# A two-model chain on one core: TensorE's queue written out by hand up to the retention stage, and attention's steps in another order

## The chip, the cores and the metric

The kernel runs on one core of one Trainium2 chip. A core has a matrix engine (TensorE, PE in the profile, with its weight loads as PEld), VectorE (DVE), ScalarE (ACT), GpSimd (POOL) and SyncE (SP), which here only issues the DMA transfers of weights. Each engine works its own queue in the order in which it was given, and waits at an instruction until what it needs is there. The metric is the device time of one execution in microseconds; less is better.

## The reference, cut to what matters

256 positions of 1024 numbers go through ten stages, all in fp32. Seven of them have a name that the text uses: f00, f01, f10, f11 (the feed-forward halves of the first model), conv, attention, and retention and f20 of the second model.

```python
for l in range(DEPTH):                     # DEPTH = 2
    g = norm_g[l]
    if l == N_A_LAYERS:                    # N_A_LAYERS = 1
        k, v = shared_kv(h, kv_norm_g, w_kv)
    h = h + 0.5 * rmsnorm(swiglu(rmsnorm(h, g[0]), ffn_w_gu[l, 0], ffn_w_down[l, 0]), g[1])
    xn = rmsnorm(h, g[2])
    if l < N_A_LAYERS:
        mix = short_gated_conv(xn, conv_w_in[l], conv_k[l], conv_w_out[l])
    else:
        mix = diff_attention(xn, k, v, attn_w_q[j], attn_lambda[j], attn_subln_g[j], attn_w_o[j], lambda_init)
    h = h + rmsnorm(mix, g[3])
    h = h + 0.5 * rmsnorm(swiglu(rmsnorm(h, g[4]), ffn_w_gu[l, 1], ffn_w_down[l, 1]), g[5])
# second model, on the result x of the first
x = x + retention(rms_norm(x, mix_norm[0]), ret_w_in[0], ret_out_norm[0], ret_w_o[0])
x = x + swiglu_2(rms_norm(x, ffn_norm[0]), ffn_w_in[0], ffn_w_out[0])
x = x + stick_breaking(rms_norm(x, mix_norm[1]), sb_w_in[0], sb_q_norm[0], sb_k_norm[0], sb_w_o[0])
x = x + swiglu_2(rms_norm(x, ffn_norm[1]), ffn_w_in[1], ffn_w_out[1])
```

In diff_attention each of 8 heads has two softmaxes; their difference weighs the values v, the result is normed per head and projected by w_o.

## The kernel before, in words

The 256 rows stand in SBUF as two halves h[0] and h[1] of 128 rows, called A and B here. All weights stream in as units of 1 MB. A unit is loaded raw by a DMA on SP's queue (three raw buffers), then split by `Weights.split` into two parts: ACT casts it to `whi` and DVE subtracts to `wlo`, each in two pieces of 128x1024. Five pairs of parts can be held. An fp32 product is made of three matmuls (whi by xT's high part, wlo by the high part, whi by the low part), lines L274 to L276 where weights stand as columns, L297 to L303 in the projections that accumulate rows (`acc`), L487 and L490 in the feed-forward's input projection `whole`. Twelve matmuls of 512 columns on one half of the rows and half a unit are called a step.

The order on PE, ACT and DVE is that of a scheduler that builds each engine's queue from the source, from its own estimates of when data are ready; only a few pieces are marked `manual_schedule` and stand as written: part of the opening, and ACT in stage 8.

Between two stages `boundary` runs: the previous stage's last steps for half A, then `chain_A[0]` (the update of h: squares on ACT, `y` on DVE L387 and L389, a power on POOL L392, `h` on DVE L394), two of the last steps for half B, `chain_A[1]` (eight transposes `tr_x` of h on PE L338 in two groups of four, which ACT L321 and DVE L323 turn into the parts xT), the last steps for B, `chain_B[0]`, some steps of the new stage for half A, `chain_B[1]`, and the rest.

In the feed-forward stages `tr(c, half)` transposes the hidden row block (`tr_h` L520; ACT and DVE make the parts hT), and `across` turns the norm factors into a row: DVE copies `spread` (L358), PE transposes it (`tr_r` L359), ACT copies `rows`. Both borrow PSUM buffers of the accumulators.

In attention `vp` projects values (four steps of it for each half), `s1` makes scores `sc` and their maxima `nm`, `s2` the exponentials `s` on ACT (L831), `s3` the weighted difference aA (half A) or aB (half B), `pv1` transposes it (`tr` on PE, `aT` on ACT L864), `pv2` multiplies with v (`tr_o` or `mm`, L874) and norms to `yo`, `tr_o` transposes that into the parts `xk` (ACT L897, DVE L898) for the output projection `out`.

Of the kernel before, what the change touches and what calls it, by code (L numbers as in the profile page):

```python
# [194 lines left out]
def tile_two_models(ctx: ExitStack, tc: tile.TileContext, a: dict):  # L195
# [66 lines left out]
    borrowed = []  # L262
# [139 lines left out]

    def boundary(prev_tail, chain_A, chain_B, head_A, head_B, few):
        for s in prev_tail[0]:
            s()
            W.pump(1)
        chain_A[0]()
        for s in prev_tail[1][:2]:  # L410
            s()
        chain_A[1]()
        if few:
            W.pump(1)
        for s in prev_tail[1][2:]:
            s()
        chain_B[0]()
        W.pump(1)
        n = 3 if few == 2 else 2
        for s in head_A[:n]:  # L420
            s()
        chain_B[1]()
        W.pump(1)
        for s in head_A[n:]:
            s()
            W.pump(1)
        for s in head_B:
            s()
            W.pump(1)

    def ffn(tag, xT, rstd, skew=True, first=None, last_stage=False, opening=False):
# [7 lines left out]
        def gu(c, half, j, last=True):  # L439
            if j == 0:  # L440
                gu_ps[c, half] = new_mm()
            mm_col(gu_ps[c, half], xT[half], (tag, "gu", c), j, last)
            if j == 1:
                evict(c, half)
# [69 lines left out]
        def tr(c, half):  # L514
            if c not in hT:
                hT[c] = k4.tile([P, 2, 2, 2, P], F32R, tag="k4", name=f"hT{c}")
            t = new_tr("tr_h")
            src = hid.pop((c, half))
            for k in range(2):
                T.transpose(t[:, k * P : k * P + P], src[:, k * P : k * P + P], ident)  # L520
            split_plain(t[:, 0:256].rearrange("p (k t) -> p k t", k=2), hT[c][:, half, 0], hT[c][:, half, 1])
# [22 lines left out]
        def body():  # L544
            nonlocal first
            if opening:
                for j in range(2):
                    by_tile(0, j)
                    W.pump()
                for j in range(2):  # L550
                    for half in range(2):
                        gu(1, half, j, last=half == 1)
                    W.pump()
                    for half in range(2):
                        borrowed.append(half)
                        if j == 0:
                            tr(0, half)
                        elif half == 0:
                            across(rstd)
                            acc.update(factors(rstd))  # L560
                        borrowed.pop()
            for c in range(2 if skew or opening else 0, NCH):
                for j in range(2):
                    whole(c, j)
                    borrowed.append(0)
                    if first is not None:
                        first()
                        first = None
                    if opening and c == 2 and j == 0:
                        tr(1, 0)  # L570
                        borrowed[-1] = 1
                        tr(1, 1)
                    if skew and c == 2 and j == 0:
                        tr(1, 1)
                    borrowed[-1] = 1
                    if not opening and c == (2 if skew else 0) and j == 0:
                        across(rstd)
                        acc.update(factors(rstd))
                    borrowed.pop()
                    W.pump()  # L580
                if 2 <= c < NCH - 1:
                    for half in range(2):
                        dn(c - 2, half, last=half == 1)
                    W.pump()
# [183 lines left out]
    def attention(xT, rstd, xk, rstd_k, kT):  # L768
# [154 lines left out]

        def body():
            vp(2, 0, 0)
            tr_q(1, 1)
            vp(2, 1, 0)
            W.pump(1)
            s1(0, 1)
            vp(2, 0, 1)  # L930
            s2(0, 1)
            vp(2, 1, 1)
            W.pump(1)
            s1(1, 1)
            s3(0, 1)
            vp(3, 0, 0)
            pv1(0, 0)
            s2(1, 1)
            vp(3, 1, 0)
            W.pump(1)  # L940
            pv2(0, 0)
            s1(2, 1)
            s3(1, 1)
            vp(3, 0, 1)
            s2(2, 1)
            pv1(1, 0)
            tr_o(0, 0)
            vp(3, 1, 1)
            W.pump(1)
            pv2(1, 0)  # L950
            s1(3, 1)
            s3(2, 1)

        def out(j, half):
            def run():
                if j == 0:
                    acc[half] = new_acc(half, f"acc{half}")
                if (j, half) == (2, 0):
                    tr_o(1, 0)
                if (j, half) == (3, 0):  # L960
                    tr_o(0, 1)
                if (j, half) == (1, 1):
                    tr_o(1, 1)
                y = yT[half]
                mm_row(
                    acc[half], (lambda k: y[0][:, k, :], lambda k: y[1][:, k, :]), 2 * j, "ao", j,
                    j == 0, j == 3, half == 1,
                )
                if half == 0:
                    if j == 0:  # L970
                        s2(3, 1)
                        pv1(0, 1)
                    elif j == 1:
                        s3(3, 1)
                        pv2(0, 1)
                    elif j == 2:
                        pv1(1, 1)
                    else:
                        pv2(1, 1)

            return run

# [356 lines left out]
    def start(make, gcols):  # L1339
        xT, rstd = {}, {}  # L1340
        stage = make(xT, rstd)
        x_t = [k4.tile([P, 4, 2, P], F32, tag="k4", name=f"x_t{g}") for g in range(2)]

        def x_load(k, n):
            Q.dma_start(x_t[k // 4][:, k % 4 : k % 4 + n], a["x_t"][:, k : k + n])

        with tc.manual_schedule(engines={mybir.EngineType.Activation}):
            S.dma_start(gains, a["gains"])
            S.activation(small(tag="t"), nhalf[:, 0:1], AF.Silu)
        ones = junk(512)  # L1350
        V.memset(ones, 1.0)
        warm = new_acc(0, "warm")[:, 0:512]
        for _ in range(WARM):
            T.matmul(warm, ones[:, 0:P], ones, start=True, stop=True)
        W.load(4, lambda p: p % 2 or x_load(p, 2))
        x_load(4, 2)
        W.load(2, lambda p: p and x_load(6, 2))
        for half in range(2):
            Q.dma_start(h[half], x[0, half * P : half * P + P])
        W.load()  # L1360
        for half in range(2):
            xT[half] = new_xT(half)
        hi, lo = (xts[-1][:, i] for i in range(2))

        def x_in(k):
            src = x_t[k // 4][:, k % 4]
            S.activation(hi[:, k], src, AF.Copy, scale=gcols[:, k : k + 1])
            V.scalar_tensor_tensor(
                lo[:, k], src, gcols[:, k : k + 1], hi[:, k].bitcast(F32), ALU.mult, ALU.subtract
            )  # L1370

        with tc.manual_schedule():
            W.split(4, lambda p: x_in(p))
            W.split(4, lambda p: x_in(4 + p))
            for half in range(2):
                rstd[half] = rms_of(half)
        return stage

    def stage(n, make, update, gcols, prev, spares=(), gb=None, few=0, end=None):

        xT, rstd = {}, {}
        ch = xchain(update, prev[1], gcols, xT, rstd)
        heads, body, tails, acc = make(xT, rstd)
        W.spares = list(spares)
        boundary(prev[0], ch[0], ch[1], heads[0], heads[1], few)
        W.spares = []
        if end is not None:
            end()
        if gb is not None:
            gbs.append(load_gb(*gb))  # L1390
        body()
        return tails, acc
# [16 lines left out]
        Q.dma_start(out[0, P : 2 * P], h[1])  # L1409

    TWO = [(0, 1), (2, 3)]
    heads, body, tails, acc = start(mk_ffn("f00", skew=False, opening=True), g_norm(0, 0))
    gbs.append(load_gb(0, 1))
    body()
# [14 lines left out]
    kT = big(2, [P, 8, 2 * P], F32, "kT")  # L1429
    heads, tr_k = kproj(xk, rstd_k, kT)  # L1430
    W.spares = [(3, 4)]
    boundary(cur[0], ch[0], ch[1], heads[0], heads[1], 0)
    W.spares = []
    gbs.append(load_gb(1, 1))
    heads, body, tails, acc = ffn("f10", xT, rstd_k, skew=False, first=lambda: tr_k(1, 1))
# [4 lines left out]
    cur = stage(5, mk_ffn("f11"), add_normed(gbs[-1], 1.0), g_norm(1, 4), cur, [(2, 3)], gb=(1, 5), few=1)  # L1440
    cur = stage(6, retention, add_normed(gbs[-1], HALF), g_cols(G_MIX, 8), cur, TWO)
    cur = stage(7, mk_ffn("f20"), add_plain, g_cols(G_FFN, 8), cur, TWO)
    act_order = tc.manual_schedule(engines={mybir.EngineType.Activation})
    act_order.__enter__()
    cur = stage(8, stick, add_plain, g_cols(G_MIX + 8, 8), cur, TWO)
# [60 lines left out]
```

## Time and profile before

| | |
|---|---|
| time, median of 3 runs | 1597.99 us (1597.76 to 1599.32) |
| time of the profiled execution | 1596.82 us |
| span of the profiled execution, first to last instruction | 1595.0 us |
| mean granted TensorE clock | 0.998 of full speed |
| PE busy | 1570.0 us, 98% of the span |
| DVE busy, ACT busy | 1088.0 us (68%), 926.8 us (58%) |

The busy rows say how full an engine's queue is, and the list of waits says what PE's idle time was ended by. With PE this full, what matters is where PE stands still and what it stands for; the time line of single instructions shows that.

### The profile page before, as it was taken

To read this page: it belongs to the slowest core of one execution; us is meant where nothing else is said; L and a number is where in the kernel's file an instruction comes from. 1 tells how busy PE (TensorE), PEld (TensorE's weight loads), DVE (VectorE), ACT (ScalarE), POOL (GpSimd) and SP (SyncE) were. 2 spreads that over 40 slices of the span, in tenths; PEclk is the share of its full clock that TensorE was granted. 3 is DMA by queue.
4 is the path that set the end of the run, shared out by engine and by line. 5 is a ranking of instruction groups with operands and counts; after the bars stand their busy time and mean duration, and the time that the engine had idled before them with its cause. 6 is when DMAs were issued, how large, how long until landed. Compare 5 with 4: busy or idle time off the path is not lost.

```text
span 1595.0 us, 21678 instructions
## 1 busy us (share of the span) xinstructions
PE 1570.0 (98%) x8395; PEld 1374.9 (86%) x8395; DVE 1088.0 (68%) x1742; ACT 926.8 (58%) x1611; POOL 61.2 (4%) x65
## 2 busy tenths in 40 slices
PE   8999999999999999989999999999999999999998
PEld 6899888899989999877899888888899988688997
DVE  6766867666677666787666776456567666666664
ACT  6655656555676555676555554556455566655552
POOL 0000100000000000001000010000000021000000
PEclk9999999999999999999999999999999999999999
DMA  8655644555545555444455555545455553235551
GB/s 331 238 211 189 247 159 175 204 203 197 211 175 205 205 196 213 148 159 163 176 202 209 203 196 185 185 158 188 164 206 203 205 205 138 101 134 210 211 193 46
DMA packets 43448, 300.94 MB, mean 189 GB/s; under 512 B 4864, under 2 KB 4992, under 8 KB 8016
## 3 DMA queue, kind: packets, MB, share of 16 engines
q1 hardware_dynamic: 42768, 297.81, 51.6%
q0 software_dynamic: 432, 1.64, 0.3%
q8 instruction: 66, 1.08, 0.3%
q14 instruction: 38, 0.31, 0.1%
q10 hardware_dynamic: 144, 0.09, 0.0%
HBM read 298.48 MB, written 1.05 MB: 188 GB/s over the span
## 4 chain that ended last, share of the span: by engine, by line
PE 86%; DVE 6%; ACT 4%; issue 1%; POOL 1%; DMA 1%; ACTq 0%; POOLq 0%
PE mm L487 24%; PE mm L490 12%; PE acc L303 8%; PE acc L297 8%; PE acc L300 8%; PE mm L276 7%; PE mm L274 7%; PE mm L275 7%; DVE wlo L172 2%; ACT whi L171 1%; PE tr L632 1%; POOL r L392 1%; PE tr_x L338 1%; DMA raw<-in_w 1%; PE z L1246 1%
## 5 line engine op out<-in xcount | busy, mean ns | idle before, releaser
L172 DVE TENSOR_TENSOR wlo<-raw,whi 128x1024 fp32r<-128x1024 f32 (+1 forms) x536 | 636.1, 1214 | 319.4 <-ACT whi L171 318.7
L171 ACT CAST whi<-raw 128x1024 fp32r<-128x1024 f32 (+1 forms) x536 | 540.4, 1045 | 332.3 <-issue 134.3
L487 PE MATMUL mm<-xT,whi 128*128 128x512 f32 x1792 | 584.0, 382 | 0.0
L490 PE MATMUL mm<-xT,wlo 128*128 128x256 f32 x1792 | 453.2, 273 | 0.0
L487 PEld LDWEIGHTS mm<-xT,whi 128*128 128x128 f32 x1792 | 326.3, 190 | 36.5
L490 PEld LDWEIGHTS mm<-xT,wlo 128*128 128x128 f32 x1792 | 342.7, 191 | 11.8
L274 PE MATMUL mm<-whi,xT 128*128 128x512 f32 x488 | 191.1, 392 | 2.0 <-ACT whi L171 1.4
L275 PE MATMUL mm<-wlo,xT 128*128 128x512 f32 x488 | 185.6, 380 | 0.7 <-DVE wlo L172 0.6
L276 PE MATMUL mm<-whi,xT 128*128 128x512 f32 x488 | 185.5, 380 | 0.0
L297 PE MATMUL acc<-whi,hT 128*128 128x512 f32 x516 | 153.9, 380 | 0.0
L303 PE MATMUL acc<-whi,hT 128*128 128x512 f32 x516 | 153.8, 379 | 0.0
L300 PE MATMUL acc<-wlo,hT 128*128 128x512 f32 x516 | 153.5, 379 | 0.0
L300 PEld LDWEIGHTS acc<-wlo,hT 128*128 128x128 f32 x516 | 97.5, 189 | 13.9
L303 PEld LDWEIGHTS acc<-whi,hT 128*128 128x128 f32 x516 | 97.5, 189 | 13.8
L297 PEld LDWEIGHTS acc<-whi,hT 128*128 128x128 f32 x516 | 97.3, 189 | 12.3 <-DVE hT L330 0.2
L274 PEld LDWEIGHTS mm<-whi,xT 128*128 128x128 f32 x488 | 92.1, 189 | 17.8 <-issue 2.3
L275 PEld LDWEIGHTS mm<-wlo,xT 128*128 128x128 f32 x488 | 92.3, 189 | 14.8 <-DVE wlo L172 2.3
L276 PEld LDWEIGHTS mm<-whi,xT 128*128 128x128 f32 x488 | 92.2, 189 | 14.2 <-DVE xT L323 1.2
L503 ACT COPY part<-mm 128x256 f32<-128x256 f32 x112 | 41.5, 371 | 55.6 <-PE mm L487 55.6
L329 ACT CAST hT<-hid 128x256 fp32r<-128x256 f32 x112 | 45.4, 405 | 26.1 <-DVE hid L511 26.1
L511 DVE TENSOR_TENSOR hid<-gated,sg 128x256 f32<-128x256 f32 x112 | 47.6, 425 | 11.8 <-ACT sg L507 3.7
L508 ACT COPY part<-mm 128x256 f32<-128x256 f32 x112 | 41.7, 372 | 19.1 <-PE mm L487 19.1
(246 smaller groups left out, 1622.6 us busy)
## 6 DMA issues: line engine op xcount, KB each, us to landing
raw<-in_w SPq DMA_DIRECT2D x276, 1024.0 KB, 4.8
gb<-in_norm_g SPq DMA_DIRECT2D x6, 512.0 KB, 5.6
x_t<-in_x_t SPq DMA_DIRECT2D x4, 256.0 KB, 5.5
raw<-in_w SPq DMA_DIRECT2D x4, 256.0 KB, 4.6
raw<-in_w SPq DMA_DIRECT2D x2, 512.0 KB, 7.0
h<-in_x SPq DMA_DIRECT2D x2, 512.0 KB, 8.4
dec<-in_decay POOLq DMA_DIRECT2D x1, 768.0 KB, 9.3
out<-h SPq DMA_DIRECT2D x1, 512.0 KB, 4.6
```

Of the source, the lines that this page charges most:

```text
L171: self.nc.scalar.copy(hi[:, c], raw[:, c])
L172: self.nc.vector.tensor_tensor(lo[:, c], raw[:, c], hi[:, c].bitcast(F32), ALU.subtract)
L274: T.matmul(o, xh, wh, start=start, stop=False)
L275: T.matmul(o, xh, wl, start=False, stop=False)
L276: T.matmul(o, xl, wh, start=False, stop=stop)
L297: T.matmul(acc[:, n * 512 : n * 512 + 512], xh(kts + k), columns(wh, c), start=st, stop=False)
L300: T.matmul(acc[:, n * 512 : n * 512 + 512], xh(kts + k), columns(wl, c), start=False, stop=False)
L303: T.matmul(acc[:, n * 512 : n * 512 + 512], xl(kts + k), columns(wh, c), start=False, stop=sp[n])
L329: S.copy(hi, tr)
L487: T.matmul(ps[n], wh[:, w], x2, start=kk == 0, stop=kk == 7, skip_group_check=True)
L490: T.matmul(o, wl[:, w], x2[:, 0], start=False, stop=False, skip_group_check=True)
L511: V.tensor_tensor(hd, t[1], sg, ALU.mult)
```

## The change

From the opening to the end of stage 7 (f20) PE's queue is held in the order of the source (`manual_schedule` for PE alone). The other engines' queues are still ordered by the scheduler. With it, some source lines move: at boundaries whose update is normed three steps of half A stand ahead of `chain_B[1]` (two elsewhere); in the opening h is loaded after the third weight unit and that unit is split ahead of the norms; the `tr` and `across` calls of f00 move; in attention the values of half A are projected first, and pv1, pv2 and tr_o stand elsewhere. No instruction is added or removed on any engine.

```diff
-    def boundary(prev_tail, chain_A, chain_B, head_A, head_B, few):
+    def boundary(prev_tail, chain_A, chain_B, head_A, head_B, few, ahead):
...
-        n = 3 if few == 2 else 2
-        for s in head_A[:n]:
+        for s in head_A[:ahead]:
             s()
         chain_B[1]()
         W.pump(1)
-        for s in head_A[n:]:
+        for s in head_A[ahead:]:
...
                     for half in range(2):
                         gu(1, half, j, last=half == 1)
+                        if j == 1:
+                            borrowed.append(half)
+                            tr(0, half)
+                            borrowed.pop()
                     W.pump()
-                    for half in range(2):
-                        borrowed.append(half)
-                        if j == 0:
-                            tr(0, half)
-                        elif half == 0:
-                            across(rstd)
-                            acc.update(factors(rstd))
-                        borrowed.pop()
...
-                    if opening and c == 2 and j == 0:
-                        tr(1, 0)
-                        borrowed[-1] = 1
-                        tr(1, 1)
+                    if opening and c == 2:
+                        tr(1, j)
...
-                    if not opening and c == (2 if skew else 0) and j == 0:
+                    if c == (2 if skew or opening else 0) and j == 0:
                         across(rstd)
...
         def body():
             vp(2, 0, 0)
+            vp(2, 0, 1)
             tr_q(1, 1)
+            pv1(0, 0)
             vp(2, 1, 0)
             W.pump(1)
             s1(0, 1)
-            vp(2, 0, 1)
+            pv2(0, 0)
             s2(0, 1)
             vp(2, 1, 1)
             W.pump(1)
             s1(1, 1)
             s3(0, 1)
             vp(3, 0, 0)
-            pv1(0, 0)
+            pv1(1, 0)
             s2(1, 1)
+            vp(3, 0, 1)
+            tr_o(0, 0)
+            s1(2, 1)
+            s3(1, 1)
             vp(3, 1, 0)
             W.pump(1)
-            pv2(0, 0)
-            s1(2, 1)
-            s3(1, 1)
-            vp(3, 0, 1)
+            pv2(1, 0)
             s2(2, 1)
-            pv1(1, 0)
-            tr_o(0, 0)
             vp(3, 1, 1)
...
-                if (j, half) == (2, 0):
-                    tr_o(1, 0)
-                if (j, half) == (3, 0):
-                    tr_o(0, 1)
-                if (j, half) == (1, 1):
-                    tr_o(1, 1)
...
                     if j == 0:
                         s2(3, 1)
+                        tr_o(1, 0)
                         pv1(0, 1)
...
                     else:
+                        tr_o(0, 1)
                         pv2(1, 1)
+                elif j == 1:
+                    tr_o(1, 1)
...
+        W.load()
         for half in range(2):
             Q.dma_start(h[half], x[0, half * P : half * P + P])
-        W.load()
...
             W.split(4, lambda p: x_in(4 + p))
+            W.split()
             for half in range(2):
                 rstd[half] = rms_of(half)
...
-        boundary(prev[0], ch[0], ch[1], heads[0], heads[1], few)
+        boundary(prev[0], ch[0], ch[1], heads[0], heads[1], few, 2 if update is add_plain else 3)
...
+    pe_order = tc.manual_schedule(engines={mybir.EngineType.PE})
+    pe_order.__enter__()
     heads, body, tails, acc = start(mk_ffn("f00", skew=False, opening=True), g_norm(0, 0))
...
     cur = stage(7, mk_ffn("f20"), add_plain, g_cols(G_FFN, 8), cur, TWO)
+    pe_order.__exit__(None, None, None)
```

The first place is in f00, on PE, behind the first `whole`. Before, `tr_h` and `tr_r` stand apart among the second `whole`'s matmuls (left out here but for the last three), and `acc` follows:

```order
L520 MATMUL tr_h<-ident,hid 128x128 x2
...
L359 MATMUL tr_r<-ident,spread 128x128 [waits DVE_49]
...
L520 MATMUL tr_h<-ident,hid 128x128 [waits Activation_49]
L520 MATMUL tr_h<-ident,hid 128x128
...
L487 MATMUL mm<-xT,whi_250 128x512
L490 MATMUL mm<-xT,wlo_251 128x256
L487 MATMUL mm<-xT,whi_250 128x512
L297 MATMUL acc_517<-whi_290,hT_332 128x512 [waits DVE_49]
```

After, PE:

```order
L520 MATMUL tr_h<-ident,hid 128x128 x2
L359 MATMUL tr_r<-ident,spread 128x128 [waits DVE_49,PE_49]
L359 MATMUL tr_r<-ident,spread 128x128 [waits DVE_49]
L490 MATMUL mm<-xT,wlo_253 128x256
...
L487 MATMUL mm<-xT,whi_252 128x512
L520 MATMUL tr_h<-ident,hid 128x128 [waits PE_49]
L520 MATMUL tr_h<-ident,hid 128x128
L297 MATMUL acc_519<-whi_292,hT_350 128x512 [waits DVE_49,Activation_49]
```

And DVE's queue after, at the same place:

```order
L330 TENSOR_TENSOR hT_421<-tr_h,hT_421 128x256 [waits Activation_49]
L358 COPY spread<-rstd_194 128x128 [waits DVE_49,Pool_49]
L172 TENSOR_TENSOR wlo_327<-raw_250,whi_326 128x1024 [waits DMAHW3_49,Activation_49]
L172 TENSOR_TENSOR wlo_327<-raw_250,whi_326 128x1024 [waits Activation_49]
L358 COPY spread<-rstd_201 128x128 [waits PE_49,Pool_49]
```

The two `tr_r` now stand next to each other behind the first `whole`'s `tr_h`, and between the two `spread` copies that they read stand two `wlo` of a weight unit; the second pair of `tr_h` moved behind the second `whole`, right ahead of `acc`.

The second place is in attention's output projection, on ACT. Before, the two copies `aT` stand ahead of the exponentials of the last score group (`s`):

```order
L864 COPY aT<-tr_6705 128x512 [waits DVE_49,PE_49]
L864 COPY aT<-tr_6712 128x512 [waits PE_49,Activation_49]
L831 ACTIVATE s,sums<-s,nm 128x256 [waits DVE_49]
L831 ACTIVATE s,sums<-s,nm 128x256 x3
L879 ACTIVATE sq<-mm 128x512 [waits PE_49,Activation_49]
```

After, ACT there:

```order
L891 ACTIVATE xk_6581<-tr_6707,gsub 128x512 [waits PE_49]
L825 ACTIVATE s,sums<-s,nm 128x256 [waits DVE_49]
L825 ACTIVATE s,sums<-s,nm 128x256 x3
L858 COPY aT<-tr_6714 128x512 [waits PE_49]
L858 COPY aT<-tr_6721 128x512 [waits PE_49,Activation_49]
```

And PE after, which these copies serve:

```order
L626 MATMUL tr_6714<-ident,aB 128x128 [waits Activation_49]
L626 MATMUL tr_6714<-ident,aB 128x128 x3
L626 MATMUL tr_6721<-ident,aB 128x128 [waits Activation_49]
L626 MATMUL tr_6721<-ident,aB 128x128 x3
L297 MATMUL acc_6689<-whi_6461,xk_6581 128x512 x2
```

The exponentials now stand ahead of both copies, and PE's second group of `aB` transposes waits for ACT.

The third place is the boundary from f11 to retention, on PE: the transposes of half A's h among the last accumulations of half B. Before:

```order
L300 MATMUL acc_7328<-wlo_8343,hT_8410 128x512 x2
L303 MATMUL acc_7328<-whi_8342,hT_8410 128x512
L338 MATMUL tr_x<-ident,h_99 128x128 [waits DVE_49,PE_49]
L338 MATMUL tr_x<-ident,h_99 128x128 x3
L338 MATMUL tr_x<-ident,h_99 128x128 [waits DVE_49,PE_49]
L338 MATMUL tr_x<-ident,h_99 128x128 x3
L303 MATMUL acc_7328<-whi_8342,hT_8410 128x512
```

After:

```order
L303 MATMUL acc_7330<-whi_8312,hT_8269 128x512 x2
L338 MATMUL tr_x<-ident,h_99 128x128 [waits DVE_49,PE_49]
L338 MATMUL tr_x<-ident,h_99 128x128 x3
L338 MATMUL tr_x<-ident,h_99 128x128 [waits DVE_49,PE_49]
L338 MATMUL tr_x<-ident,h_99 128x128 x3
L297 MATMUL acc_7330<-whi_8344,hT_8412 128x512 x2
```

One accumulation stood behind these transposes before; now twelve do.

## Rows read from the trace of the kernel before

**Rows 1.** The page's busy times, and its chain of work that ended last.

```profile
PE 1570.0 (98%) x8395; PEld 1374.9 (86%) x8395; DVE 1088.0 (68%) x1742; ACT 926.8 (58%) x1611; POOL 61.2 (4%) x65
...
PE 86%; DVE 6%; ACT 4%; issue 1%; POOL 1%; DMA 1%; ACTq 0%; POOLq 0%
```

**Rows 2.** Waits of PE: who waited for whom, total us, times, longest us.

```profile
PE tr_x L338 <- DVE h L394: 5.6, 7, 1.4
...
PE warm L1354 <- DVE uT L667: 1.5, 1, 1.5
PE mm L274 <- ACT whi L171: 1.4, 1, 1.4
PE tr_x L338 <- ACT qT L798: 1.3, 1, 1.3
...
PE mm L274 <- ACT xT L321: 0.6, 1, 0.6
```

**Rows 3.** Time line of PE in the opening: start, duration, instruction, [idle before <- releaser].

```profile
17.04 0.38 PE L276 MATMUL mm<-whi,xT 128*128 128x512 f32 x1
...
22.00 0.38 PE L276 MATMUL mm<-whi,xT 128*128 128x512 f32 x1
...
31.72 0.38 PE L487 MATMUL mm<-xT,whi 128*128 128x512 f32 x1
...
36.96 0.38 PE L520 MATMUL tr_h<-ident,hid 128*128 128x128 f32 x2
...
43.17 0.70 PE L297 MATMUL acc<-whi,hT 128*128 128x512 f32 x2
```

**Rows 4.** Time line of ACT and DVE in the opening, 37 to 46 us.

```profile
37.38 0.37 ACT L329 CAST hT<-tr_h 128x256 fp32r<-128x256 f32 x1 [1.20 <-PE tr_h L520]
...
38.96 2.00 ACT L171 CAST whi<-raw 128x1024 fp32r<-128x1024 f32 x2
...
40.29 0.23 DVE L358 COPY spread<-rstd 128x128 f32<-128x128 f32 x1 [0.77 <-PE tr_r L359]
40.43 2.35 DVE L172 TENSOR_TENSOR wlo<-raw,whi 128x1024 fp32r<-128x1024 f32 x2
42.70 0.42 DVE L330 TENSOR_TENSOR hT<-tr_h,hT 128x256 fp32r<-128x256 f32 x1
```

**Rows 5.** Time line of PE at four boundaries: the transposes of half B's h.

```profile
193.92 0.55 PE L338 MATMUL tr_x<-ident,h 128*128 128x128 f32 x3 [1.42 <-DVE h L394]
...
283.03 0.66 PE L338 MATMUL tr_x<-ident,h 128*128 128x128 f32 x4 [1.16 <-DVE h L394]
...
463.17 0.66 PE L338 MATMUL tr_x<-ident,h 128*128 128x128 f32 x4 [1.28 <-DVE h L394]
...
662.36 0.66 PE L338 MATMUL tr_x<-ident,h 128*128 128x128 f32 x4 [1.29 <-ACT qT L798]
```

**Rows 6.** Time line of PE in attention, at its longest wait.

```profile
708.89 1.09 PE L632 MATMUL tr<-ident,yo 128*128 128x128 f32 x4 [3.54 <-DVE r L883]
```

**Rows 7.** Stretches: length, busy us of five engines, PEclk (granted clock), DMA share, GB/s.

```profile
706.00:710.00 4.00, 1.11 (x5) 1.14 (x6) 1.96 (x4) 1.82 (x7) 0.82 (x1) 0.86 0.73 252
710.00:712.00 2.00, 2.00 (x6) 1.55 (x6) 1.67 (x6) 0.84 (x3) 0.00 (x0) 0.50 0.05 21
```

**Rows 8.** Time line in attention's output projection, all engines.

```profile
719.73 1.21 DVE L822 TENSOR_REDUCE nm<-s 128x4 f32<-128x1024 f32 x1
...
720.97 0.51 ACT L831 ACTIVATE s<-s,nm 128x256 f32<-128x256 f32 x1 [1.12 <-DVE nm L822]
...
740.88 0.75 DVE L898 SCALAR_TENSOR_TENSOR xk<-tr,gsub,xk 128x512 fp32r<-128x512 f32 x1
...
746.62 0.38 PE L275 MATMUL mm<-wlo,xT 128*128 128x512 f32 x1
```

**Rows 9.** Time line at the boundary from f11 to retention.

```profile
921.44 1.41 DVE L394 SCALAR_TENSOR_TENSOR h<-y,r,h 128x512 f32<-128x512 f32 x2 [0.46 <-POOL r L392]
...
922.34 1.29 PE L338 MATMUL tr_x<-ident,h 128*128 128x128 f32 x8 [0.66 <-DVE h L394]
```

More of the change, by code (lines that the diff above doesn't have):

```diff
@@ L936, in body @@
             vp(3, 0, 0)
-            pv1(0, 0)
+            pv1(1, 0)
             s2(1, 1)
+            vp(3, 0, 1)
+            tr_o(0, 0)
+            s1(2, 1)
+            s3(1, 1)
             vp(3, 1, 0)
             W.pump(1)
-            pv2(0, 0)
-            s1(2, 1)
-            s3(1, 1)
-            vp(3, 0, 1)
+            pv2(1, 0)
             s2(2, 1)
-            pv1(1, 0)
-            tr_o(0, 0)
             vp(3, 1, 1)
             W.pump(1)
-            pv2(1, 0)
             s1(3, 1)
@@ L1431, in tile_two_models @@
     W.spares = [(3, 4)]
-    boundary(cur[0], ch[0], ch[1], heads[0], heads[1], 0)
+    boundary(cur[0], ch[0], ch[1], heads[0], heads[1], 0, 3)
     W.spares = []
```

## The prediction

> **What bounds the kernel now.** I read the page first: PE is busy for 1570.0 us of a span of 1595.0, and 86% of the chain that ended last runs on it [rows 1]. An edit that adds and removes no instruction can then only move PE's idle time, 25.0 us in all, 1.5 of which is the warm-up at the start [rows 2]. So 23.5 us bounds the gain; nothing so simple bounds a loss, because a queue in a fixed order can wait where a scheduler would have put something else. The list of waits names where PE stands: mostly at `tr_x`, which waits for h at boundaries, 5.6 us in seven waits [rows 2]. The longest single one is 3.54 us in attention [rows 6]. The time line then shows what stands on ACT and DVE ahead of the thing waited for, which decides whether another order helps. The method for the new kernel is the same at every place: take each engine's new order, give each instruction the duration of its row here, and see who is late.
>
> Two rates recur. From 22.00 to 31.72 PE issues 45 matmuls of 512 columns, 0.216 us each, and from 31.72 to 36.96 one `whole`, 5.24 us [rows 3]. A transpose takes 0.11, the difference of four in 0.66 and three in 0.55 [rows 5].
>
> **Opening: +3.6.** Between 17.04 and 22.00 PE issued four matmuls and four transposes, 1.3 us of work in 4.96 [rows 3]. With the third unit ahead of h, and its split ahead of the norms, the matmuls run on: 49 of them and the transposes bring the first `whole` to 17.04 + 10.6 + 0.4 = 28.1. I take 28.75, since `tr_h` still waits for `hid` a little, so 3.0 us earlier than 31.72. It ends at 34.0, with its `tr_h` at 34.2.
>
> Now the fixed order bites. Both `tr_r` stand next, and the second reads a `spread` copy that stands on DVE behind `hT` and two `wlo`. The two casts that these need stand on ACT behind its own `hT`. From `tr_h` at 34.0: 0.42 until ACT's `hT` starts (36.96 to 37.38), 0.37 for it, 1.0 for the first cast (half of 2.00), 2.35 for two `wlo`, 0.23 for `spread` [rows 3, 4]. That is 38.4, and PE waits 4.1 us where before it had matmuls to go on with. The second `whole` then ends at 43.8. Its two `tr_h` now stand right ahead of `acc` and borrow its buffer, so the first `acc` waits until DVE has read them: 0.42 + 0.37 on ACT, another cast of 1.0, the next `hT` 0.37, and two DVE `hT` of 0.42 [rows 4] give 46.8, a wait of 2.8. Before, `acc` began at 43.17 [rows 3]. Bounds: both waits gone, -3.1; both as worked and the transposes' own wait doubled, +4.3.
>
> **Boundaries of the first model: -0.7.** The h of half B comes from its own chain on ACT, DVE and POOL, so its time stays and only what PE has to do before it changes. By the order lists, 36 matmuls stand ahead of `tr_x` at each normed boundary; before there were 33 at 193.92, 30 at 283.03 and 44 at 463.17. Three more fill 0.65 of the wait of 1.42; six more fill all of the 1.16, and 1.2 is taken [rows 5]. At 463.17 eight fewer cost 1.73, of which four transposes moved ahead give back 0.44: +1.3. At 662.36 two matmuls no longer stand between the transposes, while `qT` stays the releaser: +0.4 [rows 5]. The wait ahead of f11 is one of three that share 5.6 - 1.42 - 1.16 - 1.28 - 0.66 = 1.1 us [rows 2, 5, 9]; with eleven more matmuls ahead of it I take 0.6. So -0.65 - 1.2 + 1.3 + 0.4 - 0.6 = -0.7. Bounds: 0.9 either way.
>
> **Attention: +0.8, before any effect of the clock.** The wait of 3.54 [rows 6] goes: half A's first `yo` is made several steps earlier. What is late next is the last score group. On DVE `yo` of the second group is ready at about 711.2; behind it stand two `wlo` (2.35), two score copies and a difference (1.9 together, an estimate from this stage's time line), and `nm`, 1.21 [rows 4, 8]: 716.6. On ACT the four exponentials, 0.51 each [rows 8], now stand ahead of the copies `aT`. So PE, which reaches its second group of `aB` transposes at 712, gets its buffer only at about 719, a wait of 6.9 us, with everything in PE's queue behind it, accumulations included that need nothing from there. Then PE catches up with little in the way until half A's `tr_x`, whose buffer DVE frees with the `xk` remainder, at 740.88 + 0.75 before [rows 8]; that stays behind a `wlo`, so at about 741.5, after a wait of about 3. Four more transposes and 24 accumulations (5.9) end the projection at 747.4, against 746.62 [rows 8]. Bounds: DVE three us earlier, -2.2; both waits longer by one `wlo` of 1.2, +3.2.
>
> **f11 to retention: +1.9.** One accumulation stood behind half A's `tr_x`, twelve do now. Its h lands no earlier (DVE from 921.44, PE at 922.34 [rows 9]), so PE waits from about 919 on. Eleven matmuls are 2.4 us; 0.5 comes back, as they cover most of the 0.6 that PE waits for xT behind these transposes [rows 2, 9]. Bounds: 0 if h comes earlier, +2.9 if nothing is covered and `tr_x` of half B is late too.
>
> **At nothing:** `across` in f01, f11 and f20, whose `spread` copies of 0.23 [rows 4] are covered by a `whole`; uncovered, three cost 0.7. The later h: its first reader, the square for the norms, now stands behind the third split, and PE has 49 matmuls ahead of what needs it.
>
> **The clock: +1.6.** After the 3.54 us wait the granted clock was 0.86 over 706 to 710 and 0.50 over 710 to 712 [rows 6, 7], the lower of its two levels, 1.2 instead of 2.4 GHz. That is at least 1.1 + 2.0 = 3.1 us, half of it lost: 1.6. The waits of up to 1.42 [rows 5] left no such spell. That loss lies inside 746.62, so the terms above hold no spell for the new kernel. Of the four long waits (4.1, 6.9, 3 and 3.3) at least the longest should bring one; the bounds are 0 and 6.4.
>
> **The sum.** 3.6 - 0.7 + 0.8 + 1.9 = +5.6, with the clock +7.2: 1596.82 + 7.2 = 1604.0 for a profiled execution. That execution lies 1.2 below the median of the runs (and 1.8 above its span), so 1605.2 as a median.
>
> **Rivals.**
> The clock falls after all four long waits. For it: one such wait did it [rows 6, 7]. Against: three of the four are near or under its length, and work around them differs. 5.6 + 4 x 1.6 = +12.0, 1610.0. The Trainium skill, "TensorE: Matmul & The Clock Gate", section "HAM oscillation — how this bites in real kernels", describes a kernel that finds the clock low after every wait between its groups of matmuls; by that rule this rival is the outcome, and the trace agrees as far as its one long wait goes.
>
> No change. ACT, DVE and POOL set when h, `yo` and `xk` are ready, whatever PE's order is, and PE's waits only move. For it: the releasers in the list are all DVE and ACT [rows 2]. If DVE is 2 to 3 us earlier in attention than I have it, and no spell comes, the sum is 5.6 - 3 = +2.6: about 1600.
>
> Faster. All four long waits hang on one thing: a piece of a weight split ahead of a small instruction that PE needs (`wlo` ahead of `spread`, of the scores and of `xk`; a cast ahead of `hT`). A split needs only its raw unit and a free buffer. If these pieces run earlier, in idle time that DVE (68% busy) and ACT (58%) have [rows 1], the waits, 17 us together, could halve: 5.6 - 8.5 = -2.9, and with the boundary gains at their bound about 1594.3. It decides below some 8 us of the 17. Against it: in the opening the casts stand behind `hT`, so they cannot start before `tr_h`.
>
> **How the numbers follow.** Forecast 0.45 (its own range 1601 to 1608.5), clock 0.17, no change 0.20, faster 0.18. About 0.2%, 3.2 us, is what this kernel's measurement tells from no change: slower 0.62, same 0.20, faster 0.18. The range runs from 1595 to 1611: it takes in the clock's bound and most of the faster case.
>
> **What would show it.** In the new trace: no idle of 3.5 us near 709; idle of about 4 before the second `tr_r` near 34 and 2.8 before the first `acc` near 44; about 7 before the `aB` transposes near 712, with ACT's exponentials ending just ahead; some 3 before `tr_x` near 740 and near 919; 0.8 left at 193 and none at 283. The clock row near 720 says whether a spell came. I am wrong if PE's idle total falls below 25, above all if the splits ran ahead of the small instructions, or if waits that I did not see stand in f01, conv or f20, which I took as unchanged.

## The result, and the profile after

The changed kernel takes 1615.83 us (median of 4 runs, 1615.5 to 1617.08), the one before beside it 1598.65: a ratio of 1.0109, 95% interval 1.0092 to 1.0127. That is 17.2 us slower, where 7.2 had been forecast. The profiled execution has a span of 1613.7 us, 18.7 more than before, and a mean granted clock of 0.991.

The page's busy times show little: PE 7.8 us more than before [rows 1], with the same number of instructions. More busy time for the same work is the first hint that matmuls ran at a lower clock.

```profile
PE 1577.8 (98%) x8395; PEld 1382.7 (86%) x8395; DVE 1089.0 (67%) x1742; ACT 927.1 (57%) x1611; POOL 61.1 (4%) x65
```

The list of PE's waits names nearly all places of the prediction: total us, times, longest.

```profile
PE tr L626 <- ACT aT L858: 6.5, 1, 6.5
PE tr_x L338 <- DVE h L394: 6.1, 4, 3.0
PE tr_r L359 <- DVE spread L358: 3.9, 5, 2.3
PE tr_x L338 <- DVE xk L892: 3.2, 1, 3.2
PE acc L297 <- ACT whi L171: 2.7, 1, 2.7
PE tr_x L338 <- ACT qT L792: 1.7, 1, 1.7
...
PE tr_x L338 <- DVE ts L1030: 1.3, 1, 1.3
...
PE tr_x L338 <- issue: 1.0, 1, 1.0
```

The old 3.5 us wait in attention [rows 6] is gone and `tr_x` waits for h in four instead of seven cases [rows 2]; six new lines stand in their place. The opening's time line shows how the first of them comes about:

```profile
33.99 0.38 PE L520 MATMUL tr_h<-ident,hid 128*128 128x128 f32 x2
34.41 0.37 ACT L329 CAST hT<-tr_h 128x256 fp32r<-128x256 f32 x1 [1.90 <-PE tr_h L520]
34.67 3.88 ACT L171 CAST whi<-raw 128x1024 fp32r<-128x1024 f32 x4
...
35.52 0.46 PE L359 MATMUL tr_r<-ident,spread 128*128 128x128 f32 x2 [1.15 <-DVE spread L358]
35.76 2.36 DVE L172 TENSOR_TENSOR wlo<-raw,whi 128x1024 fp32r<-128x1024 f32 x2 [0.39 <-ACT whi L171]
38.03 0.22 DVE L358 COPY spread<-rstd 128x128 f32<-128x128 f32 x1
...
38.31 0.49 PE L359 MATMUL tr_r<-ident,spread 128*128 128x128 f32 x2 [2.33 <-DVE spread L358]
...
48.58 0.67 PE L297 MATMUL acc<-whi,hT 128*128 128x512 f32 x2 [2.65 <-ACT whi L171]
```

`tr_h` stands at 33.99 (34.0 forecast) and the second `tr_r` at 38.31 (38.4 forecast), for the reason worked out: two `wlo` between the two `spread` copies. The `acc` that began at 43.17 [rows 3] begins at 48.58, though, 1.8 us later than forecast. Between 38.31 and 45.54, where the next `tr_h` stand, PE had 5.4 us of work and took 7.2. The stretches say why. The columns after a stretch's length are busy us (instructions) of PE, PEld, DVE, ACT and POOL, then PEclk, DMA share and GB/s:

```profile
35.00:38.30 3.30, 0.46 (x2) 0.30 (x2) 2.92 (x6) 3.30 (x4) 0.00 (x0) 1.00 0.80 308
38.30:43.00 4.70, 4.69 (x19) 4.09 (x20) 4.16 (x5) 1.95 (x4) 0.00 (x0) 0.64 0.75 289
49.50:53.50 4.00, 4.00 (x12) 3.21 (x11) 1.87 (x4) 0.41 (x1) 0.00 (x0) 0.57 0.51 170
470.00:475.00 5.00, 4.24 (x23) 3.66 (x24) 3.84 (x14) 3.64 (x13) 0.17 (x1) 1.00 0.87 286
670.90:674.50 3.60, 3.60 (x11) 3.06 (x12) 2.25 (x8) 2.19 (x9) 0.26 (x1) 0.53 0.46 189
729.50:733.00 3.50, 3.47 (x12) 3.03 (x13) 3.50 (x8) 0.59 (x1) 0.00 (x0) 0.58 0.53 204
753.80:760.00 6.20, 6.18 (x17) 5.13 (x18) 3.26 (x9) 1.22 (x5) 0.00 (x0) 0.52 0.79 288
937.60:941.20 3.60, 3.56 (x14) 3.27 (x15) 2.95 (x7) 2.43 (x9) 0.00 (x0) 0.57 0.68 273
```

The first row is the wait itself, and the one from 470 follows a wait of 2.35 us that left the clock at 1.00. PE is busy nearly all through the six other stretches but runs for most of each at half its clock (mean 0.52 to 0.64), behind waits of 2.33, 2.65, 1.72, 6.54, 3.24 and 3.02 us. Such a spell loses the length of its stretch times what the clock lacks: 4.7 x 0.36 = 1.7, then 1.7, 1.7, 1.5, 3.0 and 1.5, together 11.1 us. The kernel before had one spell, of 1.6 [rows 7].

### The profile page after: what moved, and what is told of

Same layout as the page of the kernel before. It is cut to its first block, busy times and chain, and to the rows that moved or that the text cites. A ratio compares the mean times of both kernels' runs of the same rounds, so it can differ in the third digit from the quotient of the medians.

```text
span 1613.7 us, 21680 instructions
## 1 busy us (share of the span) xinstructions
PE 1577.8 (98%) x8395; PEld 1382.7 (86%) x8395; DVE 1089.0 (67%) x1742; ACT 927.1 (57%) x1611; POOL 61.1 (4%) x65
## 4 chain that ended last, share of the span: by engine, by line
PE 87%; DVE 6%; ACT 3%; issue 1%; DMA 1%; POOL 1%; SPq 0%; ACTq 0%; POOLq 0%; DVEq 0%
PE mm L487 24%; PE mm L490 12%; PE acc L297 8%; PE acc L300 8%; PE acc L303 8%; PE mm L274 7%; PE mm L275 7%; PE mm L276 7%; DVE wlo L172 2%; ACT whi L171 1%; PE tr L626 1%; DMA raw<-in_w 1%; PE tr_x L338 1%; DVE h L394 1%; POOL r L392 1%
```

## The experiments

Theory 1: the fixed order on PE makes PE stand and wait where it had other work before, and behind most of the longer waits the clock falls, which costs more than the waits' own balance. Theory 2, the rival: it is the moved lines (three steps ahead, attention's new order, the later h) that cost the time. Each run is compared with the kernel before on the same chip, 1598.2 to 1598.5 us there.

**The moves without the order, and the order without the moves.** First PE goes back to the scheduler, with all moved lines kept:

```diff
-    pe_order = tc.manual_schedule(engines={mybir.EngineType.PE})
-    pe_order.__enter__()
...
-    pe_order.__exit__(None, None, None)
```

> The changed source lines (three steps ahead, later h, moved transposes, values of half A first), but PE's queue again ordered by the scheduler. Theory 1 (the fixed order on PE makes the waits, and the clock falls behind them): the opening keeps its 3.0 us of gain and the waits of 1 to 6.5 us do not appear, 1593 to 1599. Theory 2 (the moved lines themselves cost the time): 1610 or more, with the wait before the second aB transposes still there.

Measured: 1590.42 us, 0.9947 (0.9932 to 0.9962), below the kernel before. One wait of 2.6 us for `aT` and a spell behind it remain, which theory 1 had not expected. The reverse holds the old lines in source order from stage 1 on:

```diff
     cur = tails, acc
+    pe_order = tc.manual_schedule(engines={mybir.EngineType.PE})
+    pe_order.__enter__()
     cur = stage(1, conv, add_normed(gbs[-1], HALF), g_norm(0, 2), cur, TWO, gb=(0, 3))
...
     cur = stage(7, mk_ffn("f20"), add_plain, g_cols(G_FFN, 8), cur, TWO)
+    pe_order.__exit__(None, None, None)
```

> The kernel before with its own source lines, but PE's queue held in source order from stage 1 to stage 7 (the opening stays with the scheduler). Theory 1: waits of several us in attention and at the boundary to retention, each followed by a spell at the lower clock, 1605 to 1618. Theory 2: about 1599, since no line is moved.

Measured: 1624.62 us, 1.0161 (1.0146 to 1.0176), beyond what theory 1 asked for. Its waits of PE, from the list:

```profile
PE tr_x L338 <- DVE h L394: 17.0, 7, 5.4
PE tr L632 <- DVE r L883: 5.0, 1, 5.0
PE tr L632 <- DVE yo L888: 2.4, 1, 2.4
```

In source order the old lines wait 17.0 us for h alone, three times what the scheduler's order does [rows 2]. Not each wait is followed by a spell, as theory 1 had it: behind the 2.4 for `yo` the clock stayed at 1.00. So theory 2 falls: the moved lines help under either order, and the order costs. Under the scheduler they are worth 7.8 us (1598.25 to 1590.42); with the order held from stage 1 they are worth 20.5 (1624.62 to the 1604.12 of the next run), since they put into the source part of what the scheduler had done.

**The opening given back to the scheduler.** The changed kernel, with the order entered only ahead of stage 1:

```diff
     pe_order = tc.manual_schedule(engines={mybir.EngineType.PE})
-    pe_order.__enter__()
     heads, body, tails, acc = start(mk_ffn("f00", skew=False, opening=True), g_norm(0, 0))
     gbs.append(load_gb(0, 1))
     body()
     cur = tails, acc
+    pe_order.__enter__()
```

> The changed kernel, with PE's queue held in source order only from stage 1 on, so that the scheduler orders the opening with its later h. Theory 1: the opening is at about -3 instead of +7 against the kernel before, so 1615.8 - 10 = 1606. Theory 2: the moved lines of the opening still cost most of the 7, 1611 to 1616.

Measured: 1604.12 us, 1.0039 (1.0024 to 1.0053): the fixed order in the opening alone costs 11.7 us, its two spells included. PE's time line there:

```profile
33.15 0.38 PE L520 MATMUL tr_h<-ident,hid 128*128 128x128 f32 x2
...
37.96 0.39 PE L359 MATMUL tr_r<-ident,spread 128*128 128x128 f32 x2
...
39.93 0.59 PE L297 MATMUL acc<-whi,hT 128*128 128x512 f32 x2
```

The second `tr_r` comes only 0.35 us earlier than in the changed kernel (38.31), but the second `whole` fills the time ahead of it, and `acc` begins at 39.93 instead of 48.58.

**Work in the waits, to hold the clock.** Transposes of the identity, which nobody reads, fill five of the waits, and change nothing that is computed. The helper and one of the five places:

```diff
+    def fill(n, t):
+        for _ in range(n):
+            T.transpose(t, ident, ident)
...
             for b in range(nb):
+                if (g, half, b) == (0, 1, 1):
+                    fill(50, new_mm()[:, 0:P])
                 t = tr4(
```

> The changed kernel with transposes of the identity (0.11 us each) put on PE into five of its waits: 18 before the second tr_r, 20 before the first acc, 50 before the second aB transposes, 23 before half A's second tr_x after attention, 23 before half A's tr_x at retention. Each block is a little shorter than the wait. If PE's standing still is what brings the clock down, the spells behind these five waits vanish, 1.5 to 2.8 us each, 9 together: about 1607. If the clock falls for another reason, or if the waits grow by the blocks, 1615 to 1619.

Measured: 1606.24 us, 1.0045 (1.003 to 1.006). That is 9.6 less than the changed kernel, with 134 instructions more. The stretches of this kernel behind the five filled waits (38, 46, 726, 749 and 930 us), and behind two waits that were left empty (465 and 668):

```profile
38.30:42.00 3.70, 3.39 (x22) 3.16 (x23) 3.54 (x7) 2.57 (x5) 0.00 (x0) 1.00 0.91 348
46.00:52.00 6.00, 5.61 (x30) 4.79 (x29) 3.70 (x6) 1.95 (x4) 0.00 (x0) 1.00 0.58 214
465.00:470.00 5.00, 4.17 (x15) 3.42 (x16) 3.88 (x14) 3.56 (x12) 0.00 (x0) 0.66 0.84 258
668.00:672.00 4.00, 4.00 (x14) 3.29 (x13) 2.19 (x8) 1.77 (x8) 0.00 (x0) 0.58 0.34 139
...
726.00:733.00 7.00, 6.72 (x41) 6.19 (x42) 5.26 (x13) 1.42 (x3) 0.00 (x0) 1.00 0.76 255
...
749.00:756.00 7.00, 6.84 (x34) 6.07 (x35) 5.78 (x13) 4.26 (x10) 0.00 (x0) 1.00 0.72 287
...
930.00:936.00 6.00, 5.88 (x31) 5.11 (x32) 5.96 (x14) 5.14 (x14) 0.55 (x1) 1.00 0.72 276
```

The clock stays at 1.00 behind every filled wait and falls behind the two empty ones. The waits' ends did not move much (the second aB transposes still come 7 us after the first); what is saved is the clock. The spells behind the five waits had lost 11.1 - 1.7 = 9.4. A new spell behind the empty wait of 2.35 us (465 to 470) takes back 1.7, and waits outside the filled places, above all one near 190, are 1.2 shorter; that gives the 8.9 by which the two spans differ. The Trainium skill, "TensorE: Matmul & The Clock Gate", section "HAM oscillation — how this bites in real kernels", tells of a kernel that is throttled anew after each wait between its groups of matmuls; here the trace agrees for six of the changed kernel's waits, and not for the 2.35 us before 470.66, which left the clock at 1.00 there.

**What stands ahead of the copies aT.** The changed kernel, with ACT held to put the copies first:

```diff
-                        s2(3, 1)
-                        tr_o(1, 0)
-                        pv1(0, 1)
+                        with tc.manual_schedule(engines={mybir.EngineType.Activation}):
+                            tr_o(1, 0)
+                            pv1(0, 1)
+                            s2(3, 1)
```

> The changed kernel, with the transposes' call ahead of the exponentials of the last score group and ACT held to that order there, so that on ACT the two copies aT stand ahead of the four exponentials. If ACT's order makes the 6.5 us wait before the second aB transposes, it falls under 1 us and the spell at the lower clock behind it (1.4 us lost) goes too; the weighted difference of the last group is ready at about 730, just when PE comes to it: 1615.8 - 7 = 1609. If the maximum nm on DVE sets the end anyway, the wait moves to the next aB transposes: 1613 to 1616.

Measured: 1611.98 us, 1.0091 (1.0074 to 1.0108), about half of what was expected. The wait shrank from 6.54 to 3.98 us only. ACT and PE in this run, and the stretch behind the wait:

```profile
720.88 1.98 ACT L171 CAST whi<-raw 128x1024 fp32r<-128x1024 f32 x2
...
721.28 0.60 PE L626 MATMUL tr<-ident,aB 128*128 128x128 f32 x4
722.77 1.99 ACT L171 CAST sp<-raw 128x1024 fp32r<-128x1024 f32 x2
...
724.66 0.68 ACT L891 ACTIVATE xk<-tr,gsub 128x512 fp32r<-128x512 f32 x1
725.24 0.57 ACT L858 COPY aT<-tr 128x512 f32<-128x512 f32 x1
...
725.86 1.12 PE L626 MATMUL tr<-ident,aB 128*128 128x128 f32 x4 [3.98 <-ACT aT L858]
...
725.80:730.70 4.90, 4.84 (x14) 4.02 (x15) 4.90 (x7) 2.57 (x10) 0.00 (x0) 0.51 0.53 169
```

PE is ready for the copy at 721.9, but four casts of two weight splits, and `xk`, stand on ACT ahead of it. Taking the exponentials away shortens the wait by 2.6 us, and the rest stands behind the casts and `xk`. The spell did not go either: PE works through 4.9 us at a mean clock of 0.51, where the changed kernel had worked through 3.5 at 0.58. In the two traces attention as a whole gains 2.9 us.

**Half A's transposes later, at retention.** In the changed kernel, three instead of two last steps of half B ahead of them at this boundary alone:

```diff
-        for s in prev_tail[1][:2]:
+        for s in prev_tail[1][:late]:
...
+                 2 if update is add_plain else 3, 3 if n == 6 else 2)
```

> The changed kernel, with all three last steps of half B ahead of half A's transposes at the boundary to retention alone, so that twelve accumulations stand ahead of them again. They fill 2.6 us of the 3.0 us wait, and without a long wait no spell (1.5 us lost): 1615.8 - 4 = 1611.8. If PE then waits for xT instead, as the kernel before did there for 0.6 and 0.7 us: 1613.

Measured: 1613.25 us, 1.0092 (1.0079 to 1.0106), the second of the two expectations: the wait of 3.0 falls to 0.4, but PE then waits 0.87 for xT, which the twelve accumulations had covered.

**From here on, PE with the scheduler.** The moved lines (1590.42), with ACT's order as above:

```diff
-                        s2(3, 1)
-                        tr_o(1, 0)
-                        pv1(0, 1)
+                        with tc.manual_schedule(engines={mybir.EngineType.Activation}):
+                            tr_o(1, 0)
+                            pv1(0, 1)
+                            s2(3, 1)
```

> The moved lines with PE ordered by the scheduler (1590.4 before in its own run), and ACT's copies aT ahead of the exponentials as in the other run. That kernel still waits 2.6 us for aT, 0.9 for xk, and has a spell at the lower clock behind them: 1590.4 - 4 = 1586.5. If DVE's nm sets the end there, no change: 1590.

Measured: 1588.62 us, 0.9935 (0.9923 to 0.9948), 1.8 instead of 4 less; PE still waits 3.1 us for `aT`, again behind four casts. In the profiled execution no spell follows this wait. Then the later h alone, in the kernel before:

```diff
-        for half in range(2):
-            Q.dma_start(h[half], x[0, half * P : half * P + P])
         W.load()
+        for half in range(2):
+            Q.dma_start(h[half], x[0, half * P : half * P + P])
...
             W.split(4, lambda p: x_in(4 + p))
+            W.split()
```

> The kernel before with one of the moves alone: the third weight unit loaded ahead of h and split ahead of the norms. The opening gains its 3.0 to 3.6 us (first whole 3 us earlier, nothing lost behind it, since the scheduler orders PE): 1598.3 - 3.2 = 1595. If weights or norms are late elsewhere for it, 1598 or more.

Measured: 1593.09 us, 0.9966 (0.9952 to 0.9979); the later h makes most of the moves' gain, 5.2 us by the medians and 3.8 by the profiled spans (3.2 had been expected). Then one weight split moved behind the exponentials, by leaving out the `W.pump(1)` behind the last `vp` and holding ACT's order from that `vp` to the next step:

```diff
-            vp(3, 1, 1)
-            W.pump(1)
+            out_order.__enter__()
+            vp(3, 1, 1)
             s1(3, 1)
...
+                if (j, half) == (1, 0):
+                    out_order.__exit__(None, None, None)
```

> As the run with ACT's copies aT ahead of the exponentials and PE with the scheduler (1588.6), and one weight split (two casts, 2.0 us on ACT) moved behind the exponentials. In that run PE still waits 3.1 us for aT, and two splits, four casts, stand on ACT ahead of it. If the casts make that wait, it falls to about 1.1: 1586.6. If it is set by something else, 1588.5.

Measured: 1585.84 us, 0.9916 (0.9902 to 0.993), the fastest of all, 12.6 us less than the kernel before. In its list of waits no line of PE waiting for `aT` is left, so the casts were that wait. The first lines of it:

```profile
PE tr_x L338 <- DVE h L394: 3.3, 3, 1.4
PE warm L1350 <- DVE uT L661: 1.5, 1, 1.5
PE acc L297 <- ACT xk L891: 1.4, 1, 1.4
```

The gain over the run before it is 2.8 us by the medians (1588.62 to 1585.84), but the two profiled spans, neither with a spell before the kernel's end, differ by 0.3 (1585.5 and 1585.2). Matched with each other, the later kernel gains about 2 us in attention and loses 0.8 both near 190 and at the boundary to retention. All five executions here have a mean clock of 1.000, and three of the five without the move have 0.998 or 0.999, so part of the 2.8 is likely the spell that the wait brings in some executions.

The last run was to hold the moved lines with attention's own as before. Its kernel does not do that: it has `attention` a second time, and the second one, which counts, ends in the moved lines:

```diff
+    def attention(xT, rstd, xk, rstd_k, kT):
...
         def body():
             vp(2, 0, 0)
             vp(2, 0, 1)
             tr_q(1, 1)
             pv1(0, 0)
```

> PE with the scheduler and all the moved lines except those of attention, which stand as before. The later h alone gave 1593.1 and all lines 1590.4; three steps ahead should fill some 1.5 us of the waits at 193 and 283, so 1591.5 if attention's lines are worth 1, with the 3.5 us wait and its spell near 705 back. If attention's lines carry the rest, 1593.

Measured: 1589.47 us, 0.9942 (0.9928 to 0.9956). PE's queue is the same, instruction by instruction, as with all lines moved (1590.42), so the run repeats that kernel and says nothing of attention's lines. The traces do: from ahead of attention to behind it, the kernel with all lines moved takes 2.3 us less than the one with the later h alone, in each of these two runs.

## Why the prediction was wrong in size

The direction, nearly all the places and the reasons held; the sum of the waits nearly held; the term of the clock did not. The run with filled waits separates them. Matching the same matmuls of its trace with those of the kernel before, and taking off 1.7 for each of its two spells, the delays are these:

| | forecast | measured, waits filled |
|---|---|---|
| opening, to the first acc | +3.6 | +4.0 (43.17 to 47.13) |
| boundaries before attention and the one behind it | -0.7 | -0.7 (-0.6, -0.8, +1.0, +0.4, -0.7) |
| attention | +0.8 | +1.1 |
| f11 to retention | +1.9 | +2.0 |
| sum | +5.6 | +6.4 |

The entries are medians of the delays between two boundaries, rounded. In the changed kernel itself one more wait stands at half A's `tr_x` near 190 (1.0 us): two subtractions of a weight split, here named `sp`, ran on DVE ahead of `y`, which the forecast did not have.

```profile
183.87 2.35 DVE L172 TENSOR_TENSOR sp<-raw,sp 128x1024 fp32r<-128x1024 f32 x2
...
186.14 0.68 DVE L387 TENSOR_TENSOR y<-acc,gb 128x512 f32<-128x512 f32 x1
...
189.96 1.23 PE L338 MATMUL tr_x<-ident,h 128*128 128x128 f32 x7 [1.04 <-issue]
```

The `ts` wait of 1.3 at retention was left out of the sum too, and named only as a bound. By the prediction's own rates, four transposes and 24 accumulations in attention are 5.6 us, not 5.9, which changes little.

The step that failed is "The clock: +1.6", with its bounds of 0 and 6.4. It priced one spell, of the size seen before behind 3.54 us, though it had forecast four long waits; the waits of up to 1.42 had left none. Between 1.42 and 3.54 no row decided, and five of the six spells lie behind waits in that gap (1.72 to 3.24). The bound of 6.4 assumed four spells of 1.6; there were six, and they lost 11.1. Of the 4.7 beyond the bound, 1.7 lie behind the first `acc`, a wait that the prediction had forecast as 2.8 and left out of the four, 1.7 behind the `qT` wait of 1.72, and the rest in a longer spell at 753. With 11.1 for the clock, 7.6 of the 18.7 between the spans are left for the waits, 1.2 more than with filled waits; the boundary near 190 is the one place that adds to them. The rival "the clock falls after all four long waits" (1610) was the right mechanism, counted too low.

The prediction's first step is wrong for the same reason: an edit that adds no instruction need not move PE's idle time alone. PE's busy time rose by 7.8 us, since the same matmuls took longer at half the clock.

Within attention the price and the reason were right, but the reason had a second one close behind it. The wait before the second `aB` transposes was forecast as 6.9 and measured 6.54, put down to the late maximum `nm` and the exponentials on ACT, and they do set its end:

```profile
725.75 0.69 ACT L891 ACTIVATE xk<-tr,gsub 128x512 fp32r<-128x512 f32 x1
726.93 0.51 ACT L825 ACTIVATE s<-s,nm 128x256 f32<-128x256 f32 x1 [0.49 <-DVE nm L816]
```

The casts and `xk` end on ACT only about 0.5 us before `nm`, though, so that with the exponentials out of the way 3.98 us of the wait remained. The exponentials' place ahead of the copies came from the moved `tr_o` and `pv1`, as it stands so in the scheduler's version as well.

What the change meant to do also worked where PE's order was not fixed: the later h is worth about 5 us, and the moved lines together 8 (3.8 and 6.9 by the profiled spans). The fixed order turned this into a loss of 17: 11.7 of the 25 us between the two lie in the opening, the rest behind it, 7.4 of them in attention by the traces of the two kernels that differ in the order alone from stage 1 on.

## What to carry to other kernels

Where PE is as full as here (98% busy), a queue in source order must carry other work between a transpose and the small copy on another engine that comes before it; here the scheduler had put such work there. Price each forecast wait on PE with its restart, and count every one of them: here the half clock behind the waits (11.1) cost more than the waits' own balance (7.6). Look at what stands on ACT and DVE ahead of the small instruction that PE needs, above all at pieces of weight splits, which can be moved: one split of 2.0 us moved behind the exponentials took a wait of 3.1 away, and gave 2.8 by the medians.

## What the runs showed of the hardware

The granted clock does not follow the length of a wait alone. The wait of 2.35 us at the boundary to the keys left it at 1.00 in the changed kernel (470 to 475, above), and the same wait of 2.35 was followed by 0.66 in the kernel with filled waits (465 to 470). The wait of 1.72 for `qT` was followed by a spell in both of these, but in the run that changed ACT's order alone the 2.35 brought a spell (0.72 over 469 to 475) and the 1.72 none (1.00 over 669 to 676). The wait of 2.35 in the changed kernel:

```profile
470.66 0.55 PE L338 MATMUL tr_x<-ident,h 128*128 128x128 f32 x3 [2.35 <-DVE h L394]
```

Longer waits can stay without a spell too. The wait of 3.02 at retention, followed by 0.57 in the changed kernel, left the clock at 1.00 in the run with ACT's order:

```profile
933.66 1.29 PE L338 MATMUL tr_x<-ident,h 128*128 128x128 f32 x8 [3.02 <-DVE h L394]
...
933.60:938.00 4.40, 4.30 (x23) 3.75 (x24) 4.21 (x12) 3.57 (x11) 0.20 (x1) 1.00 0.57 231
```

So did the 3.1 for `aT` with PE ordered by the scheduler and ACT's copies first. The other way round, the run with the old lines held in order has a spell in its opening, where no wait ahead is longer than 1.41, while the kernel before has the same waits there and a clock of 1.00:

```profile
21.50:25.00 3.50, 3.42 (x8) 2.79 (x9) 3.50 (x5) 3.50 (x4) 0.00 (x0) 0.51 0.74 261
```

It differs between executions of one kernel as well: with filled waits three had a mean clock of 0.997 and took 1605.9 to 1606.7 us, and one had 0.999 and took 1603.9. Transposes of the identity in the wait held the clock in all five places of the profiled execution. What decides for waits between 1.4 and 3.1 us, these runs do not settle; a price for them is a chance times a spell.
